# Attention: the division moved from the probabilities to the output, and TensorE's work in a written order

## The chip, the cores and the metric

The kernel runs on one core of a Trainium2 chip. The metric is the device time of one execution in microseconds (us), the median of several runs. The engines are TensorE (PE, matrix products and transpositions; PEld is its loading of weights), VectorE (DVE), ScalarE (ACT), GpSimd (POOL), and SyncE (SP), which issues transfers by DMA. Each engine works through its own list of instructions in order; waits between engines are semaphores.

## The reference

Two transformer blocks on 512 tokens of width 1024, with 256 context tokens in the second. The second has two layers, and in each of them an attention of the form below, with 8 heads of 64. The change is to this computation alone.

```python
def softmax_with_sink(s, sink):
    sk = jnp.broadcast_to(sink.astype(jnp.float32)[:, :, None, None], s.shape[:-1] + (1,))
    return jax.nn.softmax(jnp.concatenate([s, sk], axis=-1), axis=-1)[..., :-1]

def context_attention(q, k, v, sink=None):
    ...
    s = jnp.einsum('blkgd,bckd->bkglc', qg, k).astype(jnp.float32) * ATTN_SCALE
    p = jax.nn.softmax(s, axis=-1) if sink is None else softmax_with_sink(s, sink)
    o = jnp.einsum('bkglc,bckd->blkgd', p.astype(v.dtype), v)
    return o.reshape(bn, l, h * d)
```

Layer 0 attends over a band of the neighbouring blocks of 128 tokens and over the context, with a sink, that is one more column in the softmax's sum ("windowed"). Layer 1 has two branches ("odd attention"): branch C adds a table of biases to the scores, branch D has scores over all tokens with a scale of their own for each query. A probability is an exponential over a row's sum, so the division can be made on P before the product with V or on the product after it.

## The kernel before

A unit of attention is one tile of 128 queries and two heads (p = 0, 1). For each head `scores` multiplies the queries with the keys, which are kept as a high and a low part, into a PSUM tile `sc` of up to 768 columns; `softmax` takes the maximum on DVE (in C together with the bias), then the exponential on ACT, which writes P into SBUF and its row sums into a column. `transposed` first calls `normalised` when it comes to a head's first block: DVE adds the sink's exponential (windowed alone), takes the reciprocal of the one column of sums (L945), and P is multiplied by it (L946), head 0's by DVE and head 1's by POOL. Then PE transposes blocks of P, four to a piece, into a PSUM tile `pt`, which ACT copies to SBUF, piece 1 by DVE (`ptv`, L958). `weighted` multiplies the values with the transposed blocks (two blocks of both heads to a part) into a PSUM tile `o`; at its end ACT copies `o` out (L968).

`step` (L975) is a pipeline of three stages: it takes the next stage of every unit under way, scores of unit u, transpositions of u-1, sums of u-2, and emits their parts in turn. What it emits is not the order on an engine: a scheduler orders each engine's list by priorities, and PE's work of a unit is mixed with that of its neighbours and with what else is ready.

`odd_attention` (L1715) runs branch C, then D, four pairs of heads each, four query tiles per pair: 32 units of 6 key blocks, 12 transposed blocks in 3 pieces, 24 sum products. A fourth `step` without a new unit follows each group of four. It has three `sc` tiles, one `pt`, one `o` (`nsc`, `npt`, `no`). `windowed` (L1286) runs 24 units, in four groups of six (i = 0 to 3): two context tiles with 2 key blocks each, then four tiles with 4, 5, 5 and 4; it has two of `sc` and `pt`. It is a generator, which gives way after each unit, so that the recurrence of layer 0 is emitted between its units. Both keep P and the transposed P in rings of tiles, cut from two buffers, `hThi` and `hTlo`, that the next stage also uses for its own operands (a cast L276 writes `hThi`). PE's products go through `mm` (L322), transpositions through `tr` (L325).

## Time and profile before

| | |
|---|---|
| median of 3 runs | 3553.97 us (3551.97 to 3556.66) |
| profiled execution | 3566.74 us, its span 3565.0 us |
| busy, share of the span | PE 93%, PEld 74%, DVE 58%, ACT 37%, POOL 14% |
| windowed stage | 1647 to 1790 us of the span |
| odd attention | 2957 to 3139 us of the span |

The two stages are some 9% of the span together. The rest (projections, feed-forward, convolution, the recurrence) is not touched. An execution is read from the profile by the time that its instructions start, in us from the span's start. A matmul's end is modelled, so matmuls of one run overlap in the list, and the distance between the starts of two rows says more than the length of one.

### The profile page before, as it was taken

The numbers are of one execution on the slowest core, as the hardware profiler recorded it, in microseconds if no ns is written. First come the engines' busy times: TensorE is split into PE (matmuls) and PEld (weight loads), VectorE is DVE, ScalarE is ACT, GpSimd is POOL, SyncE is SP. The second block draws the span as 40 slices with busy tenths as digits, with TensorE's granted clock in tenths as the row PEclk, the third lists the DMA queues.
The fourth block names the chain that finished last, engine by engine and source line by source line (L and its number), as shares of the span: only waits on it lengthen the run. The fifth ranks groups of instructions, "written<-read, shape, count | busy, mean of one in ns | idle before, by whom it ended". The sixth has DMA issues, their size and how long they took to land. (4 is left out here: it accounts for less than half of the span.)

```text
span 3565.0 us, 50330 instructions
## 1 busy us (share of the span) xinstructions
PE 3316.1 (93%) x19975; PEld 2638.1 (74%) x19975; DVE 2062.1 (58%) x3796; ACT 1308.6 (37%) x2150; POOL 504.1 (14%) x274
## 2 busy tenths in 40 slices
PE   8989999878999998988888899999999989999998
PEld 5677767746776777866587897888888777778887
DVE  4674554897745557686767667433334726653334
ACT  3243333327333334443542245422222525653222
POOL 0020000540200000123343331010000103410001
PEclk9999999989999998997988799999999999999999
DMA  7645565440456333445222124661221474143332
GB/s 249 193 143 167 171 219 176 133 142 12 123 175 208 108 105 109 113 117 170 52 73 68 50 71 165 144 154 54 68 63 62 135 208 153 37 131 106 95 95 83
DMA packets 520693, 436.66 MB, mean 122 GB/s; under 512 B 91924, under 2 KB 450042, under 8 KB 518922
## 3 DMA queue, kind: packets, MB, share of 16 engines
q1 hardware_dynamic: 520458, 433.45, 40.3%
q8 instruction: 157, 2.57, 0.3%
q14 instruction: 78, 0.64, 0.1%
HBM read 368.96 MB, written 63.78 MB: 121 GB/s over the span
## 5 line engine op out<-in xcount | busy, mean ns | idle before, releaser
L301 PE MATMUL dnps<-whi_dn,hidh 128*128 128x512 f32 x1120 | 449.0, 401 | 2.4 <-ACT hidh L276 1.2
L302 PE MATMUL dnps<-wlo_dn,hidh 128*128 128x512 f32 x1120 | 445.9, 398 | 0.0
L303 PE MATMUL dnps<-whi_dn,hidl 128*128 128x512 f32 x1120 | 443.4, 398 | 1.0 <-DVE hidl L277 1.0
L289 DVE TENSOR_TENSOR wlo_dn<-wraw_dn,whi_dn 128x1024 fp32r<-128x1024 f32 x136 | 167.3, 1231 | 249.8 <-ACT whi_dn L288 249.7
L301 PE MATMUL upps<-hThi,whi_up 128*128 128x512 f32 (+1 forms) x768 | 297.8, 390 | 5.3 <-DVE hThi L276 5.3
L302 PE MATMUL upps<-hTlo,whi_up 128*128 128x512 f32 (+1 forms) x768 | 295.2, 385 | 5.3 <-DVE hTlo L277 5.3
L303 PE MATMUL upps<-hThi,wlo_up 128*128 128x512 f32 (+1 forms) x768 | 294.2, 384 | 0.0
L423 DVE TENSOR_TENSOR acc<-dnps,acc 128x512 f32<-128x512 f32 x200 | 136.9, 688 | 213.4 <-PE dnps L303 212.9
L301 PEld LDWEIGHTS dnps<-whi_dn,hidh 128*128 128x128 f32 x1120 | 211.0, 188 | 64.6 <-ACT hidh L276 5.6
L288 ACT CAST whi_dn<-wraw_dn 128x1024 fp32r<-128x1024 f32 x140 | 147.1, 1051 | 283.9 <-PE dnps L303 105.5
L302 PEld LDWEIGHTS dnps<-wlo_dn,hidh 128*128 128x128 f32 x1120 | 211.3, 189 | 53.2 <-issue 2.7
L303 PEld LDWEIGHTS dnps<-whi_dn,hidl 128*128 128x128 f32 x1120 | 210.7, 189 | 53.2 <-DVE hidl L277 3.3
L302 PE MATMUL up2ps<-hTlo,whi_ff 128*128 128x512 f32 (+1 forms) x576 | 215.8, 375 | 5.0 <-DVE hTlo L277 4.7
L301 PE MATMUL up2ps<-hThi,whi_ff 128*128 128x512 f32 (+1 forms) x576 | 213.9, 373 | 2.3 <-DVE hThi L276 2.3
L303 PE MATMUL up2ps<-hThi,wlo_ff 128*128 128x512 f32 (+1 forms) x576 | 215.4, 375 | 0.0
L289 DVE TENSOR_TENSOR wlo_up<-wraw_up,whi_up 128x1024 fp32r<-128x1024 f32 x88 | 110.6, 1257 | 141.0 <-ACT whi_up L288 141.0
L301 PEld LDWEIGHTS upps<-hThi,whi_up 128*128 128x128 f32 x768 | 147.0, 192 | 54.5 <-issue 11.9
L302 PEld LDWEIGHTS upps<-hTlo,whi_up 128*128 128x128 f32 x768 | 147.5, 192 | 42.7 <-issue 9.9
L823 POOL TENSOR_TENSOR ag<-acc,gg 128x1024 f32<-128x1024 f32 x20 | 48.7, 2437 | 904.5 <-DVE acc L423 873.3
L303 PEld LDWEIGHTS upps<-hThi,wlo_up 128*128 128x128 f32 x768 | 147.8, 193 | 28.5 <-issue 0.8
L288 ACT CAST whi_ff<-wraw_ff 128x1024 fp32r<-128x1024 f32 x64 | 67.2, 1051 | 254.1 <-PE dnps L303 209.5
L289 DVE TENSOR_TENSOR wlo_ff<-wraw_ff,whi_ff 128x1024 fp32r<-128x1024 f32 x64 | 80.6, 1260 | 130.5 <-ACT whi_ff L288 130.1
(526 smaller groups left out, 7625.3 us busy)
## 6 DMA issues: line engine op xcount, KB each, us to landing
adaw<-in_w_ada_dram SPq DMA_DIRECT2D x96, 512.0 KB
wraw_up<-in_ffn_w_up_dram SPq DMA_DIRECT2D x88, 512.0 KB
wraw_ff<-in_w_ff_dram SPq DMA_DIRECT2D x64, 512.0 KB
wraw_dn<-in_w_ff_dram SPq DMA_DIRECT2D x64, 512.0 KB
adaw<-in_ffn_ada_w_dram SPq DMA_DIRECT2D x48, 512.0 KB
wraw_dn<-in_ffn_w_down_dram SPq DMA_DIRECT2D x44, 512.0 KB
adaw<-in_mix_ada_w_dram SPq DMA_DIRECT2D x32, 512.0 KB
ab<-ab SPq DMA_DIRECT2D x32, 384.0 KB
```

The source lines that it names most:

```text
L288: nc.scalar.copy(hi, raw)
L289: (eng or nc.vector).tensor_tensor(lo, raw, hi, SUB)
L301: mm(out, a[0], b[0], start=first, stop=False)
L302: mm(out, a[0], b[1], start=False, stop=False)
L303: mm(out, a[1], b[0], start=False, stop=last)
L423: nc.vector.tensor_tensor(acc[:, t, c], p, acc[:, t, c], ADD)
L823: nc.gpsimd.tensor_tensor(ag, a, gg[:, 0 if t < NT else 1, :], MUL)
```

## The change

1. `normalised` is gone. The exponential's sums go into a tile `su` of two columns per unit, the sink's exponentials beside them. After the last piece DVE adds the sink's exponentials (windowed alone) and takes the reciprocal of both sums, spread over 64 columns each: a tile R of 128 x 128, in a ring of its own. `weighted` has PE transpose R into the second half of the `o` tile, which is now 256 columns wide; ACT copies it to SBUF; when the sums are done, DVE multiplies `o` by it, which is now what writes the unit's output.
2. Every PE instruction of the attention is issued after the one before it in the code (`tensor`), so the order is written: scores of head 0 of unit u, all sums of u-2, piece 0's transpositions of u-1, scores of head 1 of u, the other pieces of u-1. `weighted` is one part instead of several.
3. Odd attention has two `sc` tiles instead of three, and three `pt` instead of one.
4. The rings: five P of the width that the stage needs and, in the rest of that buffer, tiles R (2 in odd, 7 in windowed); eight transposed P as before.

```diff
@@ -918,11 +919,16 @@
 
         nc = self.nc
+        def tensor(f, *a, **k):
+            with self.tc.issue_after(self.behind.ins) if self.behind else nullcontext():
+                self.behind = f(*a, **k)
+
         P = [None, None]
-        nb = len(vals[0])
+        nb, ptv = len(vals[0]), self.ptv
         blocks = [(p, b) for p in range(2) for b in range(nb)]
         pieces = [blocks[i:i + 4] for i in range(0, 2 * nb, 4)]
         PT = {}
+        su = self.small.tile([128, 2, 2], F32, tag="su", name="su", bufs=5)
 
         def scores(p):
             sc = self.ps.tile([128, S + CTX], F32, tag="sc", name="sc", bufs=self.nsc)
@@ -932,87 +938,80 @@
                     first -= kh.shape[1]
                 s = sc[:, S:] if i == 0 else sc[:, first:S]
                 mk = masks if i else ()
-                self.mm(s, qs[:, p, :], kh, start=True, stop=False)
-                self.mm(s, qs[:, p, :], kl, start=False, stop=not mk)
+                tensor(self.mm, s, qs[:, p, :], kh, start=True, stop=False)
+                tensor(self.mm, s, qs[:, p, :], kl, start=False, stop=not mk)
                 for j, (c, m) in enumerate(mk):
-                    nc.tensor.matmul(s[:, c:c + 128], self.identb, m, start=False, stop=j == len(mk) - 1)
-            P[p] = self.softmax(sc[:, first:], **{x: y[p] for x, y in k.items()})
-
-        def normalised(p):
-            P[p], a, es = P[p]
-            if es is not None:
-                nc.vector.tensor_tensor(a, a, es, ADD)
-            nc.vector.reciprocal(a, a)
-            (nc.gpsimd if p else nc.vector).tensor_scalar(P[p], P[p], a, None, op0=MUL)
+                    tensor(self.mm, s[:, c:c + 128], self.identb, m, start=False, stop=j == len(mk) - 1)
+            P[p] = self.softmax(sc[:, first:], su[:, 0, p:p + 1], su[:, 1, p:p + 1], **{x: y[p] for x, y in k.items()})
 
         def transposed(i):
             pt = self.ps.tile([128, 512], F32, tag="pt", name="pt", bufs=self.npt)
             t = self.scratch("PT")
-            for p, b in pieces[i]:
-                if b == 0:
-                    normalised(p)
             for j, (p, b) in enumerate(pieces[i]):
-                self.tr(pt[:, 128 * j:128 * j + 128], P[p][:, 128 * b:128 * b + 128])
+                tensor(self.tr, pt[:, 128 * j:128 * j + 128], P[p][:, 128 * b:128 * b + 128])
                 PT[p, b] = t[:, 128 * j:128 * j + 128]
             w = slice(0, 128 * len(pieces[i]))
-            (nc.vector.tensor_copy if i in self.ptv else nc.scalar.copy)(t[:, w], pt[:, w])
-
-        def weighted(j):
-            if j == 0:
-                PT["o"] = self.ps.tile([128, 128], F32, tag="o", name="o", bufs=self.no)
-            o = PT["o"]
-            for b in range(2 * j, min(2 * j + 2, nb)):
+            (nc.vector.tensor_copy if i in ptv else nc.scalar.copy)(t[:, w], pt[:, w])
+            if i == len(pieces) - 1:
+
+                r = su[:, 0]
+                if "sink" in k:
+                    nc.vector.tensor_tensor(r, r, su[:, 1], ADD)
+                PT["r"] = self.scratch("R")
+                nc.vector.reciprocal(PT["r"].rearrange("p (g c) -> p g c", g=2), r[:, :, None].to_broadcast([128, 2, 64]))
+
+        def weighted(_):
+            both = self.ps.tile([128, 256], F32, tag="o", name="o", bufs=self.no)
+            o, rt, r = both[:, :128], both[:, 128:], PT["r"]
+            tensor(self.tr, rt, r)
+            nc.scalar.copy(r, rt)
+            for b in range(nb):
                 for p in range(2):
-                    self.mm(o[64 * p:64 * p + 64, :], vals[p][b], PT[p, b], start=b == 0, stop=b == nb - 1)
-            if 2 * j + 2 >= nb:
-                nc.scalar.copy(out, o)
-                if store:
-                    nc.sync.dma_start(*store)
-
-        active.append([[partial(f, i) for i in range(n)] for f, n in ((scores, 2), (transposed, len(pieces)), (weighted, (nb + 1) // 2))])
+                    tensor(self.mm, o[64 * p:64 * p + 64, :], vals[p][b], PT[p, b], start=b == 0, stop=b == nb - 1)
+            nc.vector.tensor_tensor(out, o, r, MUL)
+            if store:
+                nc.sync.dma_start(*store)
+
+        active.append([[partial(f, i) for i in range(n)] for f, n in ((scores, 2), (transposed, len(pieces)), (weighted, 1))])
         self.step(active)
 
     def step(self, active):
 
-        todo = [u.pop(0) for u in active]
-        active[:] = [u for u in active if u]
-        for i in range(max(map(len, todo))):
-            for t in todo:
-                if i < len(t):
-                    t[i]()
-
-    def new_scratch(self, **n):
-
-        self.ring = {}
-        for (name, k), tag in zip(n.items(), ("hThi", "hTlo")):
-            W = self.hp.tile([128, KD * S], F32, tag=tag, name=f"scratch{name}")
-            w = KD * S // k
-            self.ring[name] = [W[:, w * j:w * j + w] for j in range(k)]
+        s, t, w = ([u[0] for u in active if len(u) == n] or [[]] for n in (3, 2, 1))
+        for f in s[0][:1] + w[0] + t[0][:1] + s[0][1:] + t[0][1:]:
+            f()
+        active[:] = [u[1:] for u in active if u[1:]]
+
+    def new_scratch(self, n):
+
+        P, PT = (self.hp.tile([128, KD * S], F32, tag=tag, name=f"scratch{tag}") for tag in ("hThi", "hTlo"))
+        cut = lambda W, a, b, w: [W[:, j:j + w] for j in range(a, b, w)]
+        self.ring = dict(P=cut(P, 0, 5 * n, n), R=cut(P, 5 * n, KD * S, 128), PT=cut(PT, 0, KD * S, 512))
 
     def scratch(self, name):
         r = self.ring[name]
         r.append(r.pop(0))
         return r[-1]
 
-    def softmax(self, sc, bias=None, nsink=None, sink=None, scale=None):
+    def softmax(self, sc, sums, es, bias=None, nsink=None, sink=None, scale=None):
 
         nc, v = self.nc, self.nc.vector
         st = self.small.tile([128, 8], F32, tag="sm", name="sm", bufs=8)
-        mx, nm, sums, es = (st[:, i:i + 1] for i in range(4))
+        mx, nm, mc = (st[:, i:i + 1] for i in range(3))
         n = sc.shape[1]
         P = self.scratch("P")[:, :n]
 
         if bias is not None:
             v.tensor_tensor_reduce(sc[:, :S], sc[:, :S], bias, 1.0, -3e38, op0=ADD, op1=ALU.max, accum_out=mx)
-            v.reduce_max(es, sc[:, S:], axis=AX.X)
-            v.tensor_scalar(nm, mx, es, -1.0, op0=ALU.max, op1=MUL)
+            v.reduce_max(mc, sc[:, S:], axis=AX.X)
+            v.tensor_scalar(nm, mx, mc, -1.0, op0=ALU.max, op1=MUL)
         else:
             v.reduce_max(mx, sc, axis=AX.X, negate=True)
             v.tensor_scalar(nm, mx, scale if nsink is None else nsink, None, op0=MUL if nsink is None else ALU.min)
         nc.scalar.activation(P, sc, AF.Exp, bias=nm, accum_out=sums, scale=1.0 if scale is None else scale)
         if sink is not None:
             nc.scalar.activation(es, sink, AF.Exp, bias=nm)
-        return P, sums, es if sink is not None else None
+        return P
...
@@ -1823,7 +1822,7 @@
                 esW = ExitStack()
                 other_psum(esW, "w")
                 self.nsc, self.npt, self.no, self.npp, self.ptv = 2, 2, 1, 1, (1,)
-                self.new_scratch(P=5, PT=8)
+                self.new_scratch(3 * 128 + CTX)
                 windowed = self.windowed(st, R)
                 next(windowed)
                 rest = self.recurrence(st, R)
@@ -1864,8 +1863,8 @@
                 R = self.pool("R1", es)
                 other_psum(es, "a")
                 self.act = R
-                self.nsc, self.npt, self.no, self.ptv = 3, 1, 1, (1,)
-                self.new_scratch(P=5, PT=8)
+                self.nsc, self.npt, self.no, self.ptv, self.behind = 2, 3, 1, (1,), None
+                self.new_scratch(T2)
                 self.odd_attention(st)
                 es.close()
                 if stop in ("c", "d"):
```

PE in branch C of odd attention, before, from a head's first scores to the next head's (`sc` are scores, `pt` transpositions, `o` sums; a number tells one tile from another):

```order
L322 MATMUL sc_23991<-kh_23851,qs_23855 128x256
L322 MATMUL sc_23991<-kl_23852,qs_23855 128x256
L325 MATMUL pt_23927<-consts0_73,scratchP_23849 128x128 x4
L322 MATMUL o_23922<-scratchPT_23850,cv_22682 64x128 x7
L322 MATMUL sc_23991<-kh_23851,qs_23855 128x512
L325 MATMUL pt_23949<-consts0_73,scratchP_23849 128x128 x4
L322 MATMUL o_23978<-scratchPT_23850,cv_22682 64x128
L322 MATMUL sc_23991<-kl_23852,qs_23855 128x512
```

The same place after:

```order
L323 MATMUL sc_23954<-kh_23827,qs_23831 128x256
L323 MATMUL sc_23954<-kl_23828,qs_23831 128x256
L323 MATMUL sc_23954<-kh_23827,qs_23831 128x512
L323 MATMUL sc_23954<-kl_23828,qs_23831 128x512
L326 MATMUL o_23964<-consts0_73,scratchhThi_23825 128x128
L323 MATMUL o_23964<-scratchhTlo_23826,cv_22658 64x128 x12
L326 MATMUL pt_23980<-consts0_73,scratchhThi_23825 128x128 x4
L323 MATMUL sc_23986<-kh_23827,qs_23831 128x256
L323 MATMUL sc_23986<-kl_23828,qs_23831 128x256
L323 MATMUL sc_23986<-kh_23827,qs_23831 128x512
L323 MATMUL sc_23986<-kl_23828,qs_23831 128x512
```

A head's scores now stand in one run, the sums of a unit in one run behind the transposition of R (12 in the list are 24 in the trace), and one piece of transpositions ahead of the second head's scores.

DVE in the same branch, before (`sm` holds a head's maximum and sums):

```order
L1006 ISA sc_24191,sm_24196<-sc_24191,rpb_24076 128x512
L1006 ISA sm_24196 128x1
L1007 TENSOR_REDUCE sm_24196<-sc_24191 128x1
L945 RECIPROCAL sm_24145<-sm_24145 128x1
L1008 TENSOR_SCALAR sm_24196<-sm_24196 128x1
L945 RECIPROCAL sm_24174<-sm_24174 128x1
L958 COPY scratchPT_23850<-pt_24183 128x512
L946 TENSOR_SCALAR scratchP_23849<-scratchP_23849,sm_24174 128x768
```

And after:

```order
L954 COPY scratchhTlo_23826<-pt_24174 128x512
L1006 TENSOR_REDUCE sm_24169<-sc_24164 128x1
L1005 ISA sc_24188,sm_24193<-sc_24188,rpb_24050 128x512
L1005 ISA sm_24193 128x1
L1007 TENSOR_SCALAR sm_24169<-sm_24169 128x1
L1006 TENSOR_REDUCE sm_24193<-sc_24188 128x1
L1007 TENSOR_SCALAR sm_24193<-sm_24193 128x1
L961 RECIPROCAL scratchhThi_23825<-su_24131 128x128
L971 TENSOR_TENSOR ox_24052<-o_24198,scratchhThi_23825 128x128
```

The two reciprocals of a column and the multiplication of P have gone; one reciprocal of 128 columns and the multiplication of the output stand behind the maxima. The copy of a piece stands between a head's bias operation and its second maximum.

ACT in the same branch, before:

```order
L1012 ACTIVATE scratchP_23849,sm_23996<-sc_23991,sm_23996 128x768
L1012 ACTIVATE scratchP_23849,sm_24018<-sc_24013,sm_24018 128x768
L968 COPY ox_23859<-o_23978 128x128
L958 COPY scratchPT_23850<-pt_24028 128x512
L958 COPY scratchPT_23850<-pt_24039 128x512
```

And after:

```order
L954 COPY scratchhTlo_23826<-pt_23924 128x512
L1011 ACTIVATE scratchhThi_23825,su_23897<-sc_23898,sm_23903 128x768
L954 COPY scratchhTlo_23826<-pt_23946 128x512
L967 COPY scratchhThi_23825<-o_23964 128x128
L1011 ACTIVATE scratchhThi_23825,su_23897<-sc_23930,sm_23935 128x768
```

The copy of R (L967) and that of a piece stand ahead of the exponential of the unit's second head; before, the copy of the output stood behind both exponentials.

## Rows read from the trace of the kernel before

**Rows 1.** Timeline, ACT, copies of a unit's output, odd attention: start us, length us.

```profile
3016.22 0.27 ACT L968 COPY ox<-o 128x128 f32<-128x128 f32 x1
...
3038.63 0.28 ACT L968 COPY ox<-o 128x128 f32<-128x128 f32 x1
...
3061.74 0.27 ACT L968 COPY ox<-o 128x128 f32<-128x128 f32 x1 [0.37 <-PE o L322]
...
3082.98 0.27 ACT L968 COPY ox<-o 128x128 f32<-128x128 f32 x1 [0.43 <-PE o L322]
```

**Rows 2.** Timeline, PE, one period of branch C.

```profile
3016.45 0.36 PE L322 MATMUL sc<-kh,qs 128*128 128x256 f32 x1
...
3017.33 0.43 PE L322 MATMUL o<-scratchPT,cv 128*64 128x128 f32 x2
...
3019.49 0.60 PE L325 MATMUL pt<-consts,scratchP 128*128 128x128 f32 x4
3020.02 1.09 PE L322 MATMUL o<-scratchPT,cv 128*64 128x128 f32 x14
3021.03 0.51 PE L322 MATMUL sc<-kl,qs 128*128 128x512 f32 x1
3021.38 0.60 PE L325 MATMUL pt<-consts,scratchP 128*128 128x128 f32 x4
3021.73 0.36 PE L322 MATMUL sc<-kh,qs 128*128 128x256 f32 x1
```

**Rows 3.** Timeline, ACT, output copies at ends of groups, windowed; brackets: idle before.

```profile
1703.87 0.27 ACT L968 COPY bos<-o 128x128 f32<-128x128 f32 x1 [2.02 <-PE o L322]
...
1734.21 0.27 ACT L968 COPY bos<-o 128x128 f32<-128x128 f32 x1 [2.64 <-PE o L322]
...
1789.92 0.27 ACT L968 COPY bos<-o 128x128 f32<-128x128 f32 x1 [3.36 <-PE o L322]
```

**Rows 4.** Waits, 1734 to 1790: us in total, times, longest us.

```profile
PE pt L325 <- POOL scratchP L946: 11.0, 12, 1.8
```

**Rows 5.** Stretches, 1704 to 1734: us, PE, PEld, DVE, ACT, POOL busy, clock, DMA, GB/s.

```profile
1704.00:1734.00 30.00, 23.86 (x189) 17.66 (x189) 25.39 (x100) 16.38 (x53) 8.52 (x8) 0.94 0.27 62
```

**Rows 6.** Lines by form, 2957 to 3140: busy us, mean ns | idle before, releasers.

```profile
L946 POOL TENSOR_SCALAR scratchP<-scratchP,sm 128x768 f32<-128x768 f32 x32 | 72.1, 2254 | 195.5 <-DVE sm L945 181.6 <-DVE sm L1008 8.7 <-PE sc L322 3.0
...
L958 ACT COPY scratchPT<-pt 128x512 f32<-128x512 f32 x64 | 37.4, 584 | 45.1 <-PE pt L325 45.1
...
L322 PE MATMUL o<-scratchPT,cv 128*64 128x128 f32 x384 | 34.8, 283 | 0.0
...
L1012 ACT ACTIVATE scratchP<-sc,sm 128x768 f32<-128x768 f32 x32 | 28.9, 907 | 1.8 <-DVE sm L1008 1.5
...
L946 DVE TENSOR_SCALAR scratchP<-scratchP,sm 128x768 f32<-128x768 f32 x32 | 22.3, 696 | 0.8
L1006 DVE CUSTOM_DVE_ANT_0 sc<-sc,rpb 128x512 f32<-128x512 f32 x32 | 22.2, 695 | 6.2 <-PE sc L322 5.8
L958 DVE COPY scratchPT<-pt 128x512 f32<-128x512 f32 x32 | 22.0, 689 | 21.8 <-PE pt L325 21.7
...
L1007 DVE TENSOR_REDUCE sm<-sc 128x1 f32<-128x256 f32 x32 | 12.9, 416 | 0.1
...
L1008 DVE TENSOR_SCALAR sm<-sm 128x1 f32<-128x1 f32 x32 | 6.3, 208 | 0.2
...
L276 ACT CAST hThi<-acc 128x512 fp32r<-128x512 f32 x4 | 2.3, 622 | 0.0
```

**Rows 7.** Lines by form, DVE, the whole program.

```profile
L289 DVE TENSOR_TENSOR wlo_dn<-wraw_dn,whi_dn 128x1024 fp32r<-128x1024 f32 x136 | 167.3, 1231 | 249.8 <-ACT whi_dn L288 249.7
...
L945 DVE RECIPROCAL sm<-sm 128x1 f32<-128x1 f32 x112 | 17.5, 156 | 13.2 <-ACT scratchP L1012 12.8
...
L518 DVE SCALAR_TENSOR_TENSOR bsr<-rsps,vec_b,bsr 128x128 f32<-128x128 f32 x4 | 1.4, 342 | 0.0
```

**Rows 8.** Stretches, 2957 to 3050, the first half of odd attention.

```profile
2957.00:3050.00 93.00, 88.69 (x698) 65.20 (x697) 69.12 (x209) 55.60 (x119) 37.60 (x17) 0.98 0.36 134
```

More of the change, by code (lines that the diff above doesn't have):

```diff
@@ L1 @@
-from contextlib import ExitStack
+from contextlib import ExitStack, nullcontext
 import numpy as np
@@ L125 @@
     todo = []
+    behind = None
     nhalf = 0
```

## The prediction

> **What bounds the kernel now.** I read the stretches of the two attention stages, then the instants at which a unit's output is copied, then TensorE's (PE's) own list, and only then the mean durations.
>
> The odd stage has 32 units, four to a group, and after each group the pipeline is emptied once. In branch C a group of four takes 22.41 us (3016.22 to 3038.63); in branch D a group takes 21.24 us (3061.74 to 3082.98) [rows 1]. From the first scores of one head to the same place one unit later is 5.28 us (3016.45 to 3021.73), and no row of PE in it has an idle time before it [rows 2]. So PE's list, with its changes of kind, is what the odd stage lasts. The reader is to see there that the sums of a unit come in pieces, here one of 2 and one of 14, and that after each piece some time goes by before the next kind starts.
>
> The windowed stage is another matter. Its groups of six units take 30.34 us (1703.87 to 1734.21) and then 55.71 us for two (to 1789.92) [rows 3], while PE stands and waits directly for POOL's normalisation 11.0 us in 1734 to 1790 [rows 4]. That is a fifth of the stretch. In the group before it VectorE (DVE) is the fullest engine, 25.39 of 30 us, since the recurrence still runs there [rows 5].
>
> **The change, part by part.**
>
> *Normalisation removed.* POOL multiplies head 1's P in 2.254 us and DVE head 0's in .696 us, and both stand between an exponential and the transpositions of its piece [rows 6]. They go, and with them the wait of 11.0 us of [rows 4]. In the odd stage the gain is on DVE and POOL, which are not what ends last there.
>
> *New work per unit.* One transposition of R on PE; a copy on ScalarE (ACT) in place of the old copy of the output (.27 us in [rows 1], so nothing); on DVE a wide reciprocal, 128 columns, in place of two of one column (.156 us each), and a multiplication out of PSUM. For the multiplication I take .342 us, a 128x128 operation that reads PSUM [rows 7]. The wide reciprocal occurs nowhere in this trace. Its lower bound is the one-column .156 us, its upper bound 1.231 us, an operation over eight times the columns; I take .3 us, nearest to the .342 us of the row of equal width [rows 7]. So DVE per unit loses .70 + 2 x .16 and gains .34 + .3: less than before.
>
> The Trainium skill ("VectorE: DVE Perf Modes", section "First, the fixed hardware budget") says that a reciprocal runs as iterative-divide operations with a repeat count of 8, which points to the long end; an estimate from it would be eight cycles for each of 128 columns, about 1.1 us at the clock that the page gives (0.96 GHz), and by it the sum would be near that of rival B, below. No row here shows a wide reciprocal, so the trace neither agrees nor disagrees: the one-column row does not tell a fixed cost from a cost per column.
>
> *PE's written order, odd stage.* After the change a unit gives PE: head 0's scores, R's transposition, 24 sums, 4 transpositions, head 1's scores, 8 transpositions. From [rows 2]: one head's scores .88 us (3016.45 to 3017.33), twice, 1.76. Sums: 14 occupy 1.09 us, of which the last one's own length is .28 [rows 6], so 13 spacings in .81, .06 each, and .2 to the next kind (3020.02 to 3021.03 is 1.01): 23 x .06 + .2 = 1.58. Transpositions: four take .35 when scores follow (3021.38 to 3021.73), .53 when sums follow (3019.49 to 3020.02); at .11 each eight take .35 + .44 = .79. So .35 + .79 = 1.14, and R alone .53 - 3 x .11 = .20. Sum 1.76 + 1.58 + 1.14 + .20 = 4.68 us, against 5.28: what is saved is changes of kind.
>
> With two score tiles in place of three, head 1's scores of a unit wait until the exponential of head 1 of the unit before has read that tile. That loop is, in C [rows 6]: bias and maximum .695, the copy of piece 1 .689 that stands behind it on DVE, the context's maximum .416, the next head's bias and maximum .695, the small operation .208, the exponential .907, and the scores .88: 4.49 us. It is shorter than 4.68, so PE still sets the step, but barely. In D one maximum over all columns takes the place of the bias operation and the context's maximum; PE's list is the same, so I give D the same step.
>
> Each group ends with an emptying step, and the next begins with scores for which nothing else is ready: head 1's scores of its second unit wait for head 1's exponential of its first, .695 + .416 + .208 + .907 plus about .4 of hand-overs, 2.6 us, beside which PE has .88 + .35 of work. That is a hole of 1.4; I take 1.8 for the DVE work of the old group in between, with bounds 1.3 (what it is before: 22.41 - 4 x 5.28) and 2.6 (no cover). A group is then 4 x 4.68 + 1.8 = 20.5. C: 4 x (22.41 - 20.5) = 7.6; D: 4 x (21.24 - 20.5) = 3.0. **Odd stage -10.6.** Bounds: the loop's 4.5 and hole 1.3 give 19.3 (-20); a step of 5.0 and 2.6 give 22.6 (+6).
>
> *The same in the windowed stage.* Per key block PE needs 4.68 / 6 = .78. A group has 2 + 2 + 4 + 5 + 5 + 4 = 22 blocks, 17.2, plus 12 masks at .11, 1.3: 18.5. The two context units have 1.56 us of PE work each, less than the 2.6 of one head's softmax, so their order stalls; I add 2.5: 21. Two groups 55.71 - 42 = 13.7. In the group beside the recurrence DVE has 25.39 us of work [rows 5], so I let it fall from 30.34 only to 26, -4.3. The first group, which also waits for its loads, I leave as it is. **Windowed stage -18.0**; bounds 0 (the 11.0 us of POOL replaced by waits for the exponentials, which PE must now take in order) and -30 (18.5 in three groups). The windowed units are emitted between pieces of the recurrence; its own PE work is not in the written order and may fill holes.
>
> *Exits.* P and R lie in the buffer that the next stage casts into, and it is now held until the last multiplication. Twice: multiplication .342 for copy .27, and a cast of .622 [rows 6] that used to run before the last output: (.34 - .27 + .62) x 2 = **+1.4**. If the cast waits behind nothing else it costs 0, if two casts are held, +2.7.
>
> Sum: -10.6 - 18.0 + 1.4 = -27.2. The profiled execution took 3566.74 us: 3539.5 by its own time, and 3553.97 - 27.2 = **3526.8** by the median of the runs shown.
>
> **The rivals.**
>
> *B, a slow wide reciprocal*: 1.23 us, the upper bound. It stands on DVE ahead of the multiplication and of the next unit's maximum, so the loop of 4.49 grows by .93 and becomes 5.42, above the 5.28 that C has: C gains nothing, D about 2. In the windowed stage DVE gets .93 more per unit, 5.6 per group; I take 25 for 21 us in the two late groups (-5.7) and -2 beside the recurrence. -2 - 7.7 + 1.4 = -8.3: 3545.7. For it: nothing shows the operation fast. Against it: the DVE rows shown go by columns, .342 us at 128 and 1.231 at 1024 [rows 7]. The Trainium skill's page named above speaks for B, and no run here bears it out yet.
>
> *C, the windowed stage is held by something else* (the recurrence's DVE work, loads), so only the odd stage gains: -10.6 + 1.4 = -9.2, 3544.8. Against it: 11.0 us of direct waits in two groups where the recurrence's share is small.
>
> *D, slower: the loop of the two score tiles.* ACT's order now has R's copy (.27) and a copy of a piece (.584) [rows 1, 6] ahead of head 1's exponential, and R's copy needs PE's transposition, which needs the reciprocal. If both lie in the loop together with the slow reciprocal, it is 5.42 + .27 + .58 = 6.27, a group 25.1: 4 x 2.7 + 4 x 3.9 = +26 in the odd stage, -7.7 in the windowed, +1.4: +20, 3574. It decides from the point where the odd stage loses more than 6.3, that is a step of 5.65 where 5.45 is the mean now (43.65 / 8). For it: PE's order is fixed, so one late exponential stops everything behind it. Against it: the copies have 4.7 us per unit in which to lie elsewhere, and ACT is busy only 55.6 of 93 us [rows 8].
>
> *E, nothing comes of it:* PE's changes of kind cost the same in any order (the odd stage shows no gap to give back), and the waits for POOL become waits for exponentials: 3554.
>
> **How the numbers follow.** The forecast .64 (3507 to 3545), B .14, C .08, D .08, E .06. A measurement of this kernel tells about 0.2% from no change, 7.1 us: faster is below 3546.9, slower above 3561.1. Faster: .63 of the forecast, .09 of B, .06 of C: .78. Same: .01 + .05 + .02 + .05 = .13. Slower: D, .08, and .01 of E: .09. The range leaves out D, E and .03 of the forecast: 3507 to 3552.
>
> **What would show it.** The step between outputs in C should be 4.6 to 4.8, and PE's list without waits other than the hole after each group. The wide reciprocal at .3 speaks for the forecast, at 1.2 for B or D. POOL should have nothing left in either stage. If PE waits for the exponential of head 1 before each unit's second scores, the loop of two tiles is the bound and the order too rigid. The windowed groups should be 21 us; if they stay above 27, C or E is right.

## The result: 1.07% faster, and the profile after

The changed kernel takes 3516.57 us, median of four runs (3513.10 to 3522.19), against 3555.31 for the kernel before beside it: a ratio of 0.9893, with a 95% interval from 0.9876 to 0.9909. The forecast was 3526.8 and the range 3507 to 3552. The number was right. Most of its reasons were not: the change to the attention gives almost nothing, as the runs below show, and the gain comes from a place that the prediction left out. So it was luck that the number came out.

The page of the changed kernel, whose span was 3511.3 us, has this busy time:

```profile
PE 3228.3 (92%) x20031; PEld 2627.5 (75%) x20031; DVE 2078.5 (59%) x3716; ACT 1309.2 (37%) x2150; POOL 398.1 (11%) x218
```

The groups by line of DVE show the two new operations. The wide reciprocal, for which [rows 7] left .156 to 1.231 us open, takes .950 us, and the multiplication of the output .252 us in odd attention (the columns are busy us, mean ns | idle time before):

```profile
L961 DVE RECIPROCAL scratchhThi<-su 128x128 f32<-128x128 f32 x56 | 53.2, 950 | 19.4 <-ACT scratchhThi L1011 19.0
L971 DVE TENSOR_TENSOR ox<-o,scratchhThi 128x128 f32<-128x128 f32 x32 | 8.1, 252 | 9.2 <-PE o L323 9.0
```

**Odd attention became longer.** DVE's timeline of the changed kernel, outputs of branch C, answers to [rows 1]:

```profile
2950.28 0.29 DVE L971 TENSOR_TENSOR ox<-o,scratchhThi 128x128 f32<-128x128 f32 x1 [0.61 <-PE o L323]
...
2960.73 0.29 DVE L971 TENSOR_TENSOR ox<-o,scratchhThi 128x128 f32<-128x128 f32 x1 [0.49 <-PE o L323]
...
2970.62 0.23 DVE L971 TENSOR_TENSOR ox<-o,scratchhThi 128x128 f32<-128x128 f32 x1
...
2974.30 0.29 DVE L971 TENSOR_TENSOR ox<-o,scratchhThi 128x128 f32<-128x128 f32 x1 [0.61 <-PE o L323]
```

A group of four takes 24.02 us (2950.28 to 2974.30), and in D 23.7 to 23.8, where [rows 1] had 22.41 and 21.24. The first output of a group comes 10.45 us after the last one of the group before. PE's timeline shows what happens there:

```profile
2951.61 0.60 PE L326 MATMUL pt<-consts,scratchhThi 128*128 128x128 f32 x4
2954.48 0.53 PE L323 MATMUL sc<-kh,qs 128*128 128x256 f32 x1 [2.28 <-ACT scratchhThi L1011]
...
2955.88 1.91 PE L326 MATMUL pt<-consts,scratchhThi 128*128 128x128 f32 x8
2957.44 0.56 PE L323 MATMUL sc<-kh,qs 128*128 128x256 f32 x1
...
2958.47 0.27 PE L326 MATMUL o<-consts,scratchhThi 128*128 128x128 f32 x1
2959.09 1.53 PE L323 MATMUL o<-scratchhTlo,cv 128*64 128x128 f32 x24 [0.35 <-ACT scratchhThi L967]
...
2963.95 1.53 PE L323 MATMUL o<-scratchhTlo,cv 128*64 128x128 f32 x24 [0.35 <-ACT scratchhThi L967]
```

Head 1's scores of the second unit wait 2.28 us for the exponential that must first free their tile. The last two rows are the sums of two units that follow each other: a step without a stop is 4.86 us, with .35 of waiting in it. After the stop the granted clock is at its lower level, as the view by stretches has it (us, then busy time of PE, PEld, DVE, ACT and POOL, then the granted clock):

```profile
2951.60:2954.50 2.90, 0.62 (x6) 0.38 (x4) 1.92 (x9) 1.65 (x4) 0.00 (x0) 1.00 0.20 78
2954.50:2957.40 2.90, 2.90 (x12) 2.60 (x13) 2.09 (x4) 0.81 (x2) 0.00 (x0) 0.51 0.32 90
```

PE was busy .62 of 2.9 us, and the next 2.9 us ran at 0.51, the lower level of 1.2 GHz: eight transpositions occupy 1.91 us there, against 1.04 at the higher level. The waits in the whole stage, 2900 to 3094 (total us, times, longest), name these stops and one more, the sums that wait for ACT's copy of R in every unit:

```profile
PE sc L323 <- ACT scratchhThi L1011: 19.3, 9, 2.6
...
PE o L323 <- ACT scratchhThi L967: 14.9, 32, 0.8
```

**The dense stretches became faster.** They are not touched by the change. PE's timeline of before, and then of after, at the first and the last of 96 successive products of 512 columns in the feed-forward of the second layer:

```profile
3218.08 0.39 PE L301 MATMUL up2ps<-hThi,whi_ff 128*128 128x512 f32 x1
...
3240.25 0.39 PE L303 MATMUL up2ps<-hThi,wlo_ff 128*128 128x512 f32 x1
```

```profile
3172.19 0.40 PE L302 MATMUL up2ps<-hThi,whi_ff 128*128 128x512 f32 x1
...
3193.75 0.39 PE L304 MATMUL up2ps<-hThi,wlo_ff 128*128 128x512 f32 x1
```

The same 95 steps take 22.17 us before and 21.56 after, .2334 against .2270 us a product, both at a granted clock of 1.00. How many such products there are, PE's groups by line of before show, one of three lines of each kind:

```profile
L301 PE MATMUL dnps<-whi_dn,hidh 128*128 128x512 f32 x1120 | 449.0, 401 | 2.4 <-ACT hidh L276 1.2 <-DVE acc L423 1.0
...
L301 PE MATMUL upps<-hThi,whi_up 128*128 128x512 f32 x640 | 258.2, 403 | 0.0
...
L301 PE MATMUL up2ps<-hThi,whi_ff 128*128 128x512 f32 x448 | 176.1, 393 | 0.0
```

That is 3 x (1120 + 640 + 448) = 6624 products. By .0064 us each it is an estimated 42 us, more than the whole change gained.

### The profile page after: what moved, and what is told of

Its sections match the earlier page's. It is cut to its first block, busy times and chain, and to the rows that moved or that the text cites. A ratio compares the mean times of both kernels' runs of the same rounds, so it can differ in the third digit from the quotient of the medians.

```text
span 3511.3 us, 50256 instructions
## 1 busy us (share of the span) xinstructions
PE 3228.3 (92%) x20031; PEld 2627.5 (75%) x20031; DVE 2078.5 (59%) x3716; ACT 1309.2 (37%) x2150; POOL 398.1 (11%) x218
## 5 line engine op out<-in xcount | busy, mean ns | idle before, releaser
L304 PE MATMUL dnps<-whi_dn,hidl 128*128 128x512 f32 x1120 | 435.6, 391 | 0.7 <-DVE hidl L278 0.7
L304 PEld LDWEIGHTS upps<-hThi,wlo_up 128*128 128x128 f32 x768 | 147.4, 192 | 26.2 <-issue 0.8
```

The source lines that it names most:

```text
L304: mm(out, a[1], b[0], start=False, stop=last)
```

## The experiments

Each kernel was timed beside the kernel before. "Odd" is the time from the end of the last copy of the values (`cv`) to the start of the last output, "windowed" that from the end of the last rotary row to the start of the last output, both of one profiled execution. Among the kernels with the old attention odd is 180.2 to 180.7 us and windowed 139.0 to 142.8, so that a difference of a few us in the windowed stage says little.

| kernel | median us | ratio to before, 95% | windowed | odd |
|---|---|---|---|---|
| before | 3555 to 3559 | 1 | 141.1 | 180.4 |
| before_again | 3543.0 (one run) | | 139.8 | 180.2 |
| changed | 3516.6 | .9893 (.9876 to .9909) | 121.3 | 191.9 |
| before_pad | 3516.4 | .9885 (.9867 to .9902) | 139.2 | 180.7 |
| after_shift | 3550.3 | .9968 (.9953 to .9984) | 121.7 | 193.3 |
| align_0_0 | 3555.0 | .9988 (.9977 to .9998) | 142.8 | 180.4 |
| align_0_32 | 3563.6 | 1.0020 (1.0008 to 1.0032) | 139.0 | 180.5 |
| div_only | 3522.4 | .9891 (.9873 to .9910) | 124.8 | 187.9 |
| div_narrow | 3507.4 | .9857 (.9842 to .9872) | 125.2 | 180.0 |
| order_only | 3570.0 | 1.0034 (1.0016 to 1.0053) | 146.4 | 222.7 |
| narrow | 3510.7 | .9867 (.9845 to .9889) | 116.4 | 186.4 |
| no_drain | 3486.5 | .9804 (.9782 to .9825) | 123.0 | 164.2 |
| narrow_no_drain | 3488.4 | .9805 (.9782 to .9829) | 116.9 | 161.5 |
| early_r | 3472.1 | .9762 (.9747 to .9777) | 113.2 | 154.1 |

### Is the faster dense stretch of the execution or of the kernel?

> The kernel before, unchanged, profiled beside the others. In the two profiles at hand a matmul of 512 columns in the dense feed-forward starts every .232 us before and every .227 us after, at a granted clock of 1.00 in both, and the stretches outside the two attention stages differ by about 40 us in sum, more than the stages themselves (-26 windowed and recurrence, +12 odd). If that belongs to the execution that was profiled, this one shows .227 and a span nearer to 3552 than to 3565; if it belongs to the kernel before, it shows .232 again.

This execution took 3543.0 us, where the one on which the prediction rests took 3566.74. But the same 95 steps take 22.17 us again, as its timeline shows:

```profile
3194.00 0.39 PE L301 MATMUL up2ps<-hThi,whi_ff 128*128 128x512 f32 x1
...
3216.17 0.39 PE L303 MATMUL up2ps<-hThi,wlo_ff 128*128 128x512 f32 x1
```

So the spacing belongs to the kernel, and executions differ besides: of the 23.7 us, 14.9 lie between the windowed stage and odd attention, where the recurrence is.

### The addresses alone

The tile `su` lies in a pool that is set up before the big buffers, and takes five slots of 32 bytes per partition. In the built program this moves the activations of the dense products (`hThi` from byte 102144 to 102304; `hTlo`, `hidh` and `hidl` by as much) and not the weights (`whi_dn` at 28832). The recorded texts call the activations the moving operands. That is so in the products `up2ps<-hThi,whi_ff` alone; in the `dnps<-whi_dn,hidh` of the listing above, half of the 6624, the 512 columns are the weights, and `hidh` is what PEld loads. Both kinds became faster: the means of the three groups listed are 395, 400 and 390 ns in `before_pad`, for 401, 403 and 393. The kernel before with that and nothing else:

```diff
         self.small = self.pool("small")
+        self.small.tile([128, 2, 2], F32, tag="su", name="su", bufs=5)
```

> The kernel before with nothing changed but one unused tile of the size of su (five slots of 32 bytes), so that every later buffer lies 160 bytes higher, exactly where the changed kernel has it. In the built programs the moving operands of the dense products (hThi, hTlo, hidh, hidl) then begin at an odd multiple of 32 bytes instead of a multiple of 64; the weights stay. Theory: this shift, and not the attention, gives the .227 in place of .232 to .235 us per product of 512 columns that every changed kernel so far shows, and with it most of what the stages outside the attention gave: -20 to -35 us, 3520 to 3535, and .227 in the dense stretches. Rival: the faster spacing comes with the new attention in some other way: 0 us and .232 to .235.

It takes 3516.4 us, as much as the changed kernel. The same products in its timeline, and then in that of the changed kernel with a sixth slot (`bufs=6`):

```profile
3175.13 0.40 PE L302 MATMUL up2ps<-hThi,whi_ff 128*128 128x512 f32 x1
...
3196.69 0.39 PE L304 MATMUL up2ps<-hThi,wlo_ff 128*128 128x512 f32 x1
```

```profile
3199.99 0.40 PE L302 MATMUL up2ps<-hThi,whi_ff 128*128 128x512 f32 x1
...
3222.15 0.39 PE L304 MATMUL up2ps<-hThi,wlo_ff 128*128 128x512 f32 x1
```

> The changed kernel with a sixth slot for su, 32 bytes more: the moving operands are at multiples of 64 bytes again. Theory: the dense products go back to .232 to .235 us, and the kernel to 3537 to 3552. Rival: it stays at 3517.

21.56 us with the old attention at the new addresses, 22.16 with the new attention at others, and 3550.3 us for that kernel. The address makes the gain in either kernel. It also says what the attention is worth: at the new addresses nothing to within some 9 us (3516.6 against 3516.4, by two ratios each good to about .2%), with the activations at multiples of 64 bytes .32% (.16 to .47), some 11 us. The stages lie between: windowed -17.9 and odd +11.2 make -6.7. Not all of that reaches the end: between the two stages the changed kernel took 5.9 us more than `before_pad` (1149.6 and 1143.7), a stretch that differs by more than that between two executions of one kernel.

### Which address it is

Two kernels put 32 bytes ahead of the weights, the second one no more than that, the first one another 32 behind them:

```diff
         self.const = self.pool("const")
+        self.const.tile([128, 8], F32, name="pad0")
...
         self.small = self.pool("small")
+        self.small.tile([128, 8], F32, tag="pad1", name="pad1", bufs=1)
```

> The kernel before with an unused 32 bytes ahead of the weights' buffers and 32 more behind them. In the built program weights and moving operands of the dense products then both begin at multiples of 64 bytes; before it is weights 32 beyond a multiple and moving operands at one, in the fast kernels both 32 beyond. Theory: what counts is that both have the same place within 64 bytes: .227 us per product and about 3518. Rival: it is the moving operand's own place, 32 beyond a multiple: it stays at .232 to .235 and 3550 to 3560.

> The kernel before with 32 unused bytes ahead of the weights' buffers alone: weights at multiples of 64 bytes, moving operands 32 beyond. Theory (the same place counts): as slow as before, 3550 to 3560, .232 to .235 us. Rival (the moving operand's own place counts): .227 and about 3518.

Both rules fell. With weights and activations at multiples of 64 the first kernel takes 3555.0 us, and the run of 96 products 22.17 us:

```profile
3212.98 0.39 PE L303 MATMUL up2ps<-hThi,whi_ff 128*128 128x512 f32 x1
...
3235.15 0.39 PE L305 MATMUL up2ps<-hThi,wlo_ff 128*128 128x512 f32 x1
```

The second, activations alone off by 32, takes 3563.6, and the run of products 22.16. Of the four combinations within 64 bytes only the one with both off by 32 was fast, and it was tried at one distance alone. Whether the rule is in 64 bytes, in a larger unit, or in the distance between the two buffers stays open. One rule fits the kernels of these two sections, and no run tests it: in the fast ones weights and activations begin at the same place within 256 bytes (28832 and 102304 are both 160 beyond a multiple of 256), in the slow ones they do not (160 and 0 in the kernel before, 160 and 192 in `after_shift`, 192 and 64 in `align_0_0`, 192 and 32 in `align_0_32`). All later buffers move along with these, so that it is these operands that count is not shown either.

### Each half of the change alone

`div_only` takes the division at the output, and leaves out the written order, with the old `step`, sums in parts, and the old buffers of odd attention:

```diff
-            with self.tc.issue_after(self.behind.ins) if self.behind else nullcontext():
-                self.behind = f(*a, **k)
+            f(*a, **k)
```

> The division at the output alone (it carries the 160 bytes): no written order, the old step, sums in parts, three score tiles and one of transpositions in odd attention. Theory: the division takes away the waits for POOL in the windowed stage (11 us in its two last groups) and nothing from odd attention, whose holes after the change come from the written order; with the shift about 3510. Rival: the division's new chain (reciprocal .95 us, R's transposition and copy ahead of the sums) is what made odd attention longer: the odd stage then stays at 190 us or above, and the kernel is at or above the changed one, 3517 or more.

`order_only` keeps the order and the buffers and puts `normalised` back:

```diff
+            (nc.gpsimd if p else nc.vector).tensor_scalar(P[p], P[p], a, None, op0=MUL)
```

> The written order alone, with P normalised by DVE and POOL as before (it carries the 160 bytes and the changed buffers). Theory: in a fixed order PE must wait for POOL's 2.25 us per unit, so odd attention is longer than in the changed kernel: +10 to +30 us, 3527 to 3547. Rival: the order alone makes the change's gain and loss: within 5 us of 3517.

Against `before_pad`, which has the same addresses: the division alone gives -14.4 us in the windowed stage and +7.2 in odd attention, the order with its buffers +7.2 and +42.0. No run takes the order apart from the changed number of `sc` and `pt` tiles. The order without the division is harmful, more than I expected (3570.0 for at most 3547); over odd attention of `order_only` PE waits for POOL

```profile
PE pt L326 <- POOL scratchhThi L952: 35.7, 31, 1.8
```

where in `before_pad` such waits are 1.5 us in three, and the granted clock over the stage is 0.93 against 0.99. The two belong together: without POOL in the chain the order costs 191.9 - 187.9 = 4 us in odd attention and gives 124.8 - 121.3 = 3.5 in the windowed stage.

Whose the gain in the windowed stage is, its groups of six units show better than its length (us; in brackets the granted clock of the first group, 0.89 or more in the others):

| kernel | first group | second | two late groups |
|---|---|---|---|
| before_pad | 55.1 (0.57) | 29.9 | 54.1 |
| div_only | 47.0 (0.78) | 27.7 | 50.1 |
| div_narrow | 53.4 (0.65) | 25.0 | 46.9 |
| changed | 45.1 (0.81) | 32.3 | 43.9 |
| narrow | 47.5 (0.82) | 26.2 | 42.7 |

In the two late groups the division alone gives 4.0 us, and the order with it another 6.2. The first group goes with its clock: with the same division it takes 47.0 us at 0.78 and 53.4 at 0.65. Why the clock differs there is not shown, so how much of the first group's gain is the division's stays open.

My theory that the division takes nothing from odd attention fell: it is +7.2 there without any order. The next run says why.

### The wide reciprocal

```diff
-                nc.vector.reciprocal(PT["r"].rearrange("p (g c) -> p g c", g=2), r[:, :, None].to_broadcast([128, 2, 64]))
+                nc.vector.reciprocal(r, r)
+                nc.vector.tensor_copy(PT["r"].rearrange("p (g c) -> p g c", g=2), r[:, :, None].to_broadcast([128, 2, 64]))
```

> The division alone (3522; odd attention 187.9 us there, 180.7 in the padded kernel before) with the narrow reciprocal. Theory: the .95 us of the wide reciprocal on DVE is what makes odd attention longer in it: it falls to about 181, -7 us, and the windowed stage by some more. Rival: the detour of R over PE and ACT ahead of the sums is what costs: no more than -2 us.

> The changed kernel with the reciprocal taken over the two columns of sums and a copy that spreads them, in place of one reciprocal of 128 x 128 (.95 us in the profile of the changed kernel). DVE loses about .5 us per unit. Theory: the reciprocal is not in the loop that sets the odd step, only DVE's fullness beside the recurrence (29.3 of 32.3 us) counts: -3 to -8 us. Rival: the slow reciprocal is in the loop: 56 units by .5, up to -25 us.

With the scheduler's order, odd attention falls from 187.9 to 180.0 us, where it was before the change. The rows by line of `div_only`, and then of `div_narrow`, odd attention, show what was exchanged:

```profile
L960 DVE RECIPROCAL scratchhThi<-su 128x128 f32<-128x128 f32 x32 | 30.4, 949 | 0.8
```

```profile
L961 DVE COPY scratchhThi<-su 128x128 f32<-128x128 f32 x32 | 7.1, 222 | 0.5
L960 DVE RECIPROCAL su<-su 128x2 f32<-128x2 f32 x32 | 5.0, 157 | 0.3 <-ACT scratchhThi L1017 0.3
```

.157 + .222 in place of .949 us: .57 per unit, 18 us in 32 units, of which 7.9 were on the path. That the windowed stage would gain too did not show in its length (125.2 for 124.8): its last three groups are 5.9 us shorter and its first 6.4 longer, at the lower clock.

With the written order the same edit (`narrow`) gives 5.5 in odd attention and 4.9 in the windowed stage, and the whole kernel moved by 5.9 by the medians. In the windowed stage it is the second group, beside the recurrence, that gained (32.3 to 26.2). In odd attention it is not the reciprocal's length: a step without a stop is no shorter by it, as the next section shows, and the stops are as before, 2.0 to 2.3 us after each of seven groups. But in the changed kernel the low clock follows every one of the seven, in `narrow` three. Here are two such stops of `narrow`, each with the stretch behind it:

```profile
2924.00:2926.90 2.90, 0.62 (x6) 0.39 (x4) 1.91 (x9) 1.67 (x4) 0.00 (x0) 1.00 0.23 78
2926.90:2929.80 2.90, 2.62 (x17) 2.07 (x17) 2.21 (x7) 1.38 (x3) 0.00 (x0) 1.00 0.34 90
2946.80:2949.70 2.90, 0.64 (x5) 0.36 (x3) 1.92 (x8) 1.61 (x4) 0.00 (x0) 0.99 0.23 88
2949.70:2952.60 2.90, 2.88 (x11) 2.58 (x12) 1.49 (x5) 0.85 (x2) 0.00 (x0) 0.50 0.30 90
```

Over the whole stage the granted clock is 0.96 in `narrow` and 0.94 in the changed kernel. Whether the edit brings that about or chance is not shown by one profile of each.

### The emptying after each group

```diff
-                self.step(active)
+        self.step(active)
         self.step(active)
```

(The first of the two steps out of the loop over pairs of heads.)

> The changed kernel without the emptying step after each group of four in odd attention: the units of all eight groups follow each other. Theory: odd attention became longer by the change because the emptying, with the written order, makes PE wait for head 1's exponential (2.3 to 2.9 us) and then run at the lower clock; a group takes 24.0 us where four steps of 4.87 are 19.5. Seven times 4.5 are 31 us: about 3486. Rival: the loop of two score tiles is what holds PE, and the hole only moves into the steps: 0 to -8 us.

Odd attention falls by 27.7 us to 164.2, the kernel to 3486.5, 30.1 less than the changed kernel. The outputs follow in even steps of 4.86 us, as in DVE's timeline:

```profile
3025.80 0.23 DVE L971 TENSOR_TENSOR ox<-o,scratchhThi 128x128 f32<-128x128 f32 x1
3030.66 0.23 DVE L971 TENSOR_TENSOR ox<-o,scratchhThi 128x128 f32<-128x128 f32 x1
```

So the rival, by which the two score tiles would hold every step, fell. The hole was the cost: the 19.3 us of waits seen above are 4.5 in two here,

```profile
PE sc L323 <- ACT scratchhThi L1011: 4.5, 2, 2.9
```

and the granted clock over the stage is 0.98 in place of 0.94. That accounts for some 23 of the 27.7 us, by an estimate from these numbers: 14.8 of waits, and 8 of clock (.06 of 191.9 us less .02 of 164.2).

> Both edits together. Theory: they add, about -35 us to the changed kernel (3482). If the hole after each group hid the reciprocal, more than the sum; if both edits take away the same wait, less.

The two did not add in the medians (3488.4), though both stages are shorter, odd attention by 2.7 us and the windowed stage by 6.1. In odd attention the reciprocal takes nothing off a step: the outputs follow each other after 4.91 us, with the wide one after 4.86, and it loses 2.2 us by that; it is the first group, ahead of these, that is 4.9 us shorter.

```profile
3043.42 0.29 DVE L972 TENSOR_TENSOR ox<-o,scratchhThi 128x128 f32<-128x128 f32 x1 [0.18 <-PE o L323]
3048.33 0.29 DVE L972 TENSOR_TENSOR ox<-o,scratchhThi 128x128 f32<-128x128 f32 x1 [0.18 <-PE o L323]
```

What differs besides is the recurrence that follows the windowed stage: over 320 us from its end, the granted clock was 0.92 in the profile of `no_drain` and 0.86 in this one, and the stretch from the windowed stage to odd attention took 18.7 us more. Over all kernels that clock was 0.86 to 0.92, and 0.86 and 0.90 in two executions of the kernel before. Whether a quicker windowed stage brings it about can't be said from one profile of each.

### The copy of R

`early_r` is `narrow_no_drain` with R's transposition and copy as a part of their own, ahead of head 0's scores:

```diff
-        for f in s[0][:1] + w[0] + t[0][:1] + s[0][1:] + t[0][1:]:
+        for f in w[0][:1] + s[0][:1] + w[0][1:] + t[0][:1] + s[0][1:] + t[0][1:]:
```

> The kernel without emptying and with the narrow reciprocal (3488), and R's transposition moved ahead of head 0's scores, so that ACT's copy of it is done while PE works on them; in the changed kernel the sums wait .35 us for that copy in every unit. Theory: the wait goes, a step of odd attention falls from 4.9 to about 4.55 us: -11 us there, -4 in the windowed stage, about 3473. Rival: the loop of the two score tiles is then what holds the step at 4.8 or above: 0 to -4 us.

It takes 3472.1 us, the fastest here: 1.3% less than the changed kernel and 2.4% less than before. PE's timeline of branch C:

```profile
2944.70 1.53 PE L323 MATMUL o<-scratchhTlo,cv 128*64 128x128 f32 x24
...
2947.47 1.04 PE L326 MATMUL pt<-consts,scratchhThi 128*128 128x128 f32 x8
2948.34 0.27 PE L326 MATMUL o<-consts,scratchhThi 128*128 128x128 f32 x1
...
2948.92 0.39 PE L323 MATMUL sc<-kl,qs 128*128 128x512 f32 x1
2949.40 1.53 PE L323 MATMUL o<-scratchhTlo,cv 128*64 128x128 f32 x24
```

R's transposition now stands ahead of the scores. A step is 4.70 us in C and 4.59 in D, not the 4.55 that I expected of it. A part of the wait is left: the sums start .48 us after the last product of the scores, where scores follow each other after .23, and the loading of their first weights still waits for ACT's copy of R in each of the 30 units from 2910 to 3050:

```profile
PEld o L323 <- ACT scratchhThi L968: 16.0, 30, 1.0
```

Odd attention is 7.4 us shorter than without this edit, the windowed stage 3.7.

## Why the prediction was right

**The forecast in a sentence.** -27.2 us was forecast and about -39 measured, in the same direction and inside the range. But the sum was made of windowed -18.0, odd -10.6 and exits +1.4, and the runs show windowed -17.9, odd +11.2 and the addresses -40. Two of the three terms that count were wrong: one had the wrong sign, the other was not there at all. The three measured ones make -46.7; the recurrence between the stages (+5.9) and the differences between executions take up the rest. That the number is inside the range is luck. Of the exits, that of odd attention came about as described: the first product of the next stage starts 1.0 us after the start of the last output, in `before_pad` .1 ahead of it, 1.1 for .7; behind the windowed stage no cast follows within 8 us.

**The step that was missing.** "The change, part by part" does not mention the tile `su`: it stands in the sum at nothing. That it moves the dense operands by 160 bytes was worth 1.1% (`before_pad`, .9885). The time outside the attention was not priced, since no instruction of it changes. No row of before could have told the amount; that the tile is set up ahead of the buffers of the activations could be read from the kernel.

**The windowed stage, right in sum.** -18.0 forecast, 139.2 - 121.3 = -17.9 measured. DVE's and ACT's timelines give the ends, first of `before_pad`, then of the changed kernel:

```profile
1632.46 0.69 DVE L915 TENSOR_TENSOR row<-row,rope 128x512 f32<-128x512 f32 x1
...
1772.31 0.27 ACT L969 COPY bos<-o 128x128 f32<-128x128 f32 x1 [3.37 <-PE o L323]
```

```profile
1629.58 0.69 DVE L915 TENSOR_TENSOR row<-row,rope 128x512 f32<-128x512 f32 x1
...
1751.59 0.29 DVE L971 TENSOR_TENSOR bos<-o,scratchhThi 128x128 f32<-128x128 f32 x1 [1.45 <-PE o L323]
```

Its parts came out otherwise, and that they make the same sum is luck. The two late groups took 43.9 us where I said 42, from 54.1 in `before_pad`: -10.2 for -13.7. The first group, which I left as it was, gained 10.0, and goes with its clock; in `before_pad`, and then in the changed kernel:

```profile
1633.20:1688.30 55.10, 47.29 (x318) 34.52 (x318) 26.58 (x91) 22.33 (x67) 16.26 (x18) 0.57 0.56 172
```

```profile
1630.30:1675.40 45.10, 32.03 (x321) 25.25 (x322) 27.97 (x77) 22.14 (x68) 6.84 (x11) 0.81 0.69 209
```

The second, beside the recurrence, lost 2.4 where I gave it -4.3, because the wide reciprocal falls into a stretch where DVE is the fullest engine [rows 5]; with the narrow one it takes 26.2 us, what I had said (26). The wait for POOL of [rows 4] went, as forecast, and a smaller one came, for R's copy; the waits of `before_pad` from 1720 to 1772 and of the changed kernel from 1701 to 1751:

```profile
PE pt L326 <- POOL scratchP L947: 9.9, 11, 1.8
```

```profile
PE o L323 <- ACT scratchhThi L967: 4.8, 13, 0.5
```

**Odd attention, wrong in sign.** Three terms were mis-sized, and the hole made most of the miss.

- *The hole after each group.* I took 1.8 us with bounds of 1.3 and 2.6. The first output of a group came 10.45 us after the one before, where an undisturbed step is 4.86: 5.6 more, of which the group's short last step gives 1.2 back. As the prediction counts it, four steps and a hole, the hole was 24.02 - 4 x 4.86 = 4.6. The wait itself was 2.0 to 2.3 us, inside the bounds. What I left out is the lower clock after it, though the price of a stop could be looked for in any stretch with a low clock.
- *The sums behind R's copy.* I counted R's transposition on PE and called the copy on ACT free. But in PE's written order the sums stand right behind the transposition and wait .35 us for the copy, in each of 32 units, 14.9 us in all with longer ones. Without it the step of 4.86 would be 4.51.
- *The reciprocal.* .950 us for my .3. In odd attention it did not cost what it is longer: it is beside the path in the written order (a step of 4.86 with it, 4.91 with the narrow one and its copy), and on it in the scheduler's (`div_narrow`). I chose by width, from the rows of other operations of DVE, and the row of one column showed no price per column. From two columns (.157) to 128 (.950) it is .0063 us per column, against some .001 between the 128 and the 1024 columns of [rows 7]. The Trainium skill's rule ("VectorE: DVE Perf Modes", section "First, the fixed hardware budget"), that a reciprocal is an iterative divide with a repeat count of 8, was the better guide. The estimate from it was 1.1 us, and the measured .950 stands.

**PE's list.** The sum of 4.68 us for PE's work in a unit was near, and somewhat too long: the changed kernel's step is 4.51 without its wait, with 1.56 us for two heads' scores (my 1.76), 1.46 for the sums (1.58), 1.21 for the transpositions of P (1.14) and .28 for R's (.20). That `early_r` makes 4.70 is no proof of 4.68, since a wait is left in it. That the written order takes changes of kind off PE's list, which was the core of the odd term, is so: 4.51 for 5.28. The changed kernel does not get at it, because it waits elsewhere.

**The rivals.** B (a slow reciprocal) came true as a fact, but not its mechanism: it was to lengthen the loop of the score tiles to 5.42 us, and the step is 4.86 with the slow reciprocal in it. D, slower by the loop of two score tiles, was the right kind of fear for the odd stage (+26 forecast, +11.2 measured), with the wrong place: the tiles hold PE only where the pipeline has been emptied, as `no_drain` shows. E said that the change gives nothing, and for the attention that is what is left: -11 to 0 us.

## What to carry to other kernels

A number that comes out right proves no step: here a term of -40 us that nobody had counted covered one that had the wrong sign, and only the kernel before with the addresses of the kernel after told them apart. The same holds one level down: read the granted clock of a stretch before its length is credited to an edit. Where a change adds a tile, even of a few bytes, compare a stretch that it does not touch; if that moved, pad the old kernel before crediting the change. A written order needs the pipeline kept full and every producer well ahead, since each late one stops all that stands behind it.

## What the runs showed of the hardware

- The same product of 512 columns, with the same clock and the same neighbours, started every .2270 us or every .2334 us depending on nothing but steps of 32 bytes in where the buffers lie in SBUF; over the kernel 1.1% (`before_pad` against before). Which condition on the addresses it is stays open.
- A reciprocal on DVE costs .157 us for 2 columns and .950 for 128. A copy that spreads 2 columns to 128 costs .222.
- A stop of PE of 2.28 us was followed by 2.9 us at a granted clock of 0.51, and eight transpositions occupied 1.91 us there in place of 1.04. Stops of 2.0 to 2.3 us were followed by the lower clock in seven of seven places in the changed kernel and in three of seven in `narrow`.
- In the recurrence, which no edit touched, the granted clock over 320 us was between 0.86 and 0.92 from one profiled kernel to another, and 0.86 and 0.90 in two executions of the kernel before.
